# A decoder block's delta-rule inverse: the product of its steps in a piece of the attention's memory instead of a scratch tile

## The chip, the cores and the metric

The kernel runs on one core of a Trainium2 chip. The metric is the device time of one launch in microseconds (us). Engines go by these names: TensorE (PE; PEld is its weight load), VectorE (DVE), ScalarE (ACT), GpSimd (POOL) and SyncE (SP, which issues most DMAs).

## The reference

One decoder block on x [256, 1024] in float32: one wide input projection, a gated delta rule (8 heads of 128, chunks of 64 tokens), a sparse attention with compressed, selected and windowed keys (8 query heads, 2 key heads), a gated merge of the two branches, a layer norm, a gated feed-forward with a causal convolution, and a second layer norm. The part that the change touches is the delta rule's triangular solve:

```python
lower = jnp.where(strict, jnp.einsum('nbhid,nbhjd->nbhij', k_beta, k) * decay, 0.0)
a_mat = lower + jnp.eye(C, dtype=jnp.float32)
rhs = jnp.concatenate([v_beta, k_beta * jnp.exp(g)[..., None]], -1)
sol = lax.linalg.triangular_solve(a_mat, rhs, left_side=True, lower=True, unit_diagonal=True)
```

There are 32 matrices `a_mat` (8 heads, 4 chunks) of 64x64. `v` comes from a causal convolution of four taps over the tokens and a SiLU.

## The kernel before

**Weight chunks.** The whole block is a list of weight chunks of 128x1024 (`plan`, from `head_plan`): first those of `k`, `q`, the compression and the attention's keys and queries, then eight each of `v`, `z`, `mgd`, `mgn`, `wd`, `wn`, `wo`, then the feed-forward. SyncE loads them into six `raw` buffers (L170). Each is split into a rounded part `hi` (a cast on ScalarE, L192) and a remainder `lo` (a subtraction on VectorE, L197; for a few early chunks partly on GpSimd); up to three split chunks are held. `mm_feat` (L319 to L321) multiplies a chunk of projection weights in 24 matmuls, three for each of eight 128-row slices: hi by the high half of the input, hi by its low half, lo by the high half. The result goes into a PSUM tile `pg`, of which there are two.

**What follows a `v` chunk.** `feat` multiplies and then calls `evac_v` (from L1049). It takes a scratch tile `cv` (`scr`, three buffers of 128x512 that go round in the order of the requests), and `conv` fills it: the last tap is a scaled copy on ScalarE (L146, `cv<-pg`), the three others are multiply-adds on VectorE (L351), all reading `pg`. A deferred SiLU on ScalarE then writes `cv` into `Z` (`Z<-cv`, L146). After that `feat` splits the next chunk (`ahead`) and gives every open side stream one step (`pump`).

**Side streams.** The delta rule (`delta`), the attention and others are Python generators. Each runs until it yields, and the numbers in `W` and `WAITS` say for how many chunks it does. So the order of instructions on each engine is fixed when the program is written; an engine that waits holds all that stands behind it in its queue. Waits between engines come from the tiles that the instructions read and write.

**The inverse.** `delta` inverts the diagonal 16x16 blocks of all matrices at once by substitution on GpSimd. The blocks are brought into a layout with one block row per partition by a write to DRAM and a read back (L571, L573). Then 15 steps follow, each a product into `tmp` (L581) and a subtraction from the inverse `Xi` (L583); the largest product has 8x8 = 64 elements per partition. A copy makes the transpose (L586). Two writes to DRAM (L589) and two reads (L592), transpose first, bring both into the layout for TensorE. Four masked copies each on ScalarE (L146, `LT<-VN`) and VectorE (L602) spread them into the block-diagonal `TT` (transpose, first) and `T`. From there TensorE doubles the blocks to 32 and 64: `pa` (L615, reads `L` and `TT`), `pu` (L621) and `pt` (L626). `tmp` is a scratch tile of the same three buffers, named `itmp`:

```python
tmp = self.scr("itmp")
...
t = tmp[:, :n * m].rearrange("p (r c) -> p r c", r=n)
nc.gpsimd.tensor_tensor(t, Ln[:, j + 1:16, j:j + 1].to_broadcast([128, n, m]),
                        Xi[:, 0, j:j + 1, 0:m].to_broadcast([128, n, m]), op=OP.mult)
nc.gpsimd.tensor_tensor(Xi[:, 0, j + 1:16, 0:m], Xi[:, 0, j + 1:16, 0:m], t, op=OP.subtract)
```

The requests for scratch tiles around it are, in this order: `hp` (L784, the first compression's result), `itmp`, `hp` (the second's), and one `cv` for each of the eight `v` chunks.

**AT.** A tile of 128x4608 that many parts use in turn: at first the input, then columns 0 to 4095 as slots for the compression's weight chunks (L239), the columns from 4096 on as slots for the squares of `q` and `k` (`norm_sq`), and later the attention's weights, in 0 to 4515 (`EE`, `PT`, `e6`, `er`).

Of the kernel before, what the change touches and what calls it, by code (L numbers as in the profile page):

```python
# [99 lines left out]
class Body:  # L100
# [363 lines left out]
    def delta(self):  # L464
# [106 lines left out]
        nc.gpsimd.dma_start(sl.rearrange("u p j -> p u j"), Lc)  # L571
        yield from self.wait("lw")
        nc.gpsimd.dma_start(vf[:, 256:512], sl.rearrange("u (b i) j -> (u b) (i j)", b=8))  # L573
        tmp = self.scr("itmp")
        nc.vector.memset(Xi[:, 0], 0.0)
        nc.vector.memset(vf[:, 512:768:17], 1.0)
        yield from self.wait("inv")
# [945 lines left out]
```

## Time and profile before

| what | us |
|---|---|
| median of 3 runs | 573.6 (573.47 to 574.25) |
| the profiled execution, device time | 573.08 |
| its span in the profile | 571.3 |
| TensorE busy | 554.5 (97%) |
| VectorE busy | 394.1 (69%) |
| ScalarE busy | 306.7 (54%) |
| GpSimd busy | 110.3 (19%) |

Times in the profile count from the span's start. A row of a timeline is: start, duration, engine, line, operation, output<-inputs with shapes, and in brackets the idle time of the engine ahead of it with what ended that. A wait for several engines is put down to the one that the profile shows last. Consecutive matmuls overlap, so a matmul of 0.28 us starts 0.12 us after the one ahead of it. A row of windows has the stretch, its length, then busy time and number of instructions of PE, PEld, DVE, ACT and POOL, the granted clock, the DMA engines' busy share and GB/s. [...]

### The profile page before, as it was taken

To read this page: it belongs to the slowest core of one execution; us is meant where nothing else is said; L and a number is where in the kernel's file an instruction comes from. 1 tells how busy PE (TensorE), PEld (TensorE's weight loads), DVE (VectorE), ACT (ScalarE), POOL (GpSimd) and SP (SyncE) were. 2 spreads that over 40 slices of the span, in tenths; PEclk is the share of its full clock that TensorE was granted. 3 is DMA by queue.
4 is the path that set the end of the run, shared out by engine and by line. 5 is a ranking of instruction groups with operands and counts; after the bars stand their busy time and mean duration, and the time that the engine had idled before them with its cause. 6 is when DMAs were issued, how large, how long until landed. Compare 5 with 4: busy or idle time off the path is not lost.

```text
span 571.3 us, 11612 instructions
## 1 busy us (share of the span) xinstructions
PE 554.5 (97%) x4585; PEld 508.8 (89%) x4585; DVE 394.1 (69%) x683; ACT 306.7 (54%) x575; POOL 110.3 (19%) x160
## 2 busy tenths in 40 slices
PE   8999999999799999999999999999999999999994
PEld 6999999988798898888898898899999999999974
DVE  2888745766686563467657487788777777778884
ACT  4656544624464446564677344465655555556651
POOL 2466632017401130004001000068000000000003
PEclk9999999999899999999999999999999999999998
DMA  8985548765552233223354645735655555555601
GB/s 317 406 305 180 190 146 278 287 211 185 145 182 93 76 112 111 76 73 112 112 185 128 242 148 183 258 102 180 209 185 191 191 180 192 186 189 172 200 3 73
DMA packets 28182, 99.94 MB, mean 175 GB/s; under 512 B 3340, under 2 KB 3996, under 8 KB 27740
## 3 DMA queue, kind: packets, MB, share of 16 engines
q1 hardware_dynamic: 27312, 95.94, 49.1%
q0 software_dynamic: 672, 2.93, 1.7%
q8 instruction: 36, 0.59, 0.4%
q10 hardware_dynamic: 144, 0.33, 0.1%
q14 instruction: 18, 0.15, 0.1%
HBM read 97.33 MB, written 1.46 MB: 173 GB/s over the span
## 4 chain that ended last, share of the span: by engine, by line
PE 77%; DVE 9%; ACT 6%; POOL 3%; issue 2%; DMA 2%; POOLq 0%; SPq 0%; DVEq 0%; ACTq 0%
PE pg L319 18%; PE pg L321 17%; PE pg L320 17%; PE pdn L1284 3%; PE pdn L1285 3%; PE pdn L1283 3%; DVE lo L197 2%; ACT hi L192 2%; PE poa L959 2%; PE pwo L1002 1%; PE pwo L1001 1%; PE pwo L1000 1%; ACT AT L146 1%; POOL itmp L581 1%; POOL VN L583 1%
## 5 line engine op out<-in xcount | busy, mean ns | idle before, releaser
L197 DVE TENSOR_TENSOR lo<-raw,hi 128x1024 fp32r<-128x1024 f32 (+1 forms) x147 | 179.2, 1221 | 75.3 <-ACT hi L192 74.4
L192 ACT CAST hi<-raw 128x1024 fp32r<-128x1024 f32 (+1 forms) x151 | 154.6, 1028 | 36.5 <-PE pg L320 9.8
L319 PE MATMUL pg<-X,hi 128*128 128x256 f32 x496 | 144.3, 291 | 4.8 <-ACT cv L146 4.8
L321 PE MATMUL pg<-X,lo 128*128 128x256 f32 x496 | 140.3, 283 | 0.0
L320 PE MATMUL pg<-X,hi 128*128 128x256 f32 x496 | 140.2, 283 | 0.0
L319 PE MATMUL pg<-Y,hi 128*128 128x256 f32 x400 | 113.0, 283 | 0.0
L320 PE MATMUL pg<-Y,hi 128*128 128x256 f32 x400 | 112.7, 282 | 0.0
L321 PE MATMUL pg<-Y,lo 128*128 128x256 f32 x400 | 112.5, 281 | 0.0
L319 PEld LDWEIGHTS pg<-X,hi 128*128 128x128 f32 x496 | 94.1, 190 | 9.7 <-ACT cv L146 4.9
L320 PEld LDWEIGHTS pg<-X,hi 128*128 128x128 f32 x496 | 94.2, 190 | 0.3 <-issue 0.2
L321 PEld LDWEIGHTS pg<-X,lo 128*128 128x128 f32 x496 | 94.1, 190 | 0.1
L320 PEld LDWEIGHTS pg<-Y,hi 128*128 128x128 f32 x400 | 75.3, 188 | 0.3 <-issue 0.2
L319 PEld LDWEIGHTS pg<-Y,hi 128*128 128x128 f32 x400 | 75.3, 188 | 0.2 <-issue 0.2
L321 PEld LDWEIGHTS pg<-Y,lo 128*128 128x128 f32 x400 | 75.3, 188 | 0.0
L351 DVE SCALAR_TENSOR_TENSOR cv<-pg,ppk,cv 128x255 f32<-128x255 f32 (+2 forms) x72 | 34.6, 481 | 17.4 <-ACT cv L146 15.7
L1359 POOL TENSOR_TENSOR NQ<-NQ,AT 128x512 f32<-128x512 f32 x2 | 2.6, 1298 | 159.7 <-ACT NQ L146 159.7
L1284 PE MATMUL pdn<-lo,X 128*128 128x512 f32 (+1 forms) x90 | 31.6, 351 | 0.0
L1283 PE MATMUL pdn<-hi,X 128*128 128x512 f32 (+1 forms) x90 | 31.5, 350 | 0.0
L1285 PE MATMUL pdn<-hi,X 128*128 128x512 f32 (+1 forms) x90 | 31.4, 349 | 0.0
L910 POOL TENSOR_SCALAR AT<-AT,sums 128x128 f32<-128x128 f32 (+1 forms) x12 | 10.9, 918 | 95.3 <-DVE ec L903 48.4
L351 DVE SCALAR_TENSOR_TENSOR uv<-pg,ppk,uv 128x255 f32<-128x255 f32 (+1 forms) x44 | 21.2, 481 | 11.3 <-ACT uv L146 10.1
L146 ACT ACTIVATE cv<-pg,ppk 128x256 f32<-128x256 f32 x24 | 11.4, 474 | 32.2 <-PE pg L321 26.4
(353 smaller groups left out, 925.8 us busy)
## 6 DMA issues: line engine op xcount, KB each, us to landing
raw<-in_w SPq DMA_DIRECT2D x156, 512.0 KB, 3.4
AT<-in_w SPq DMA_DIRECT2D x12, 512.0 KB, 6.4
Z<-in_w SPq DMA_DIRECT2D x4, 512.0 KB, 7.8
AT<-in_first SPq DMA_DIRECT2D x3, 512.0 KB, 6.6
V<-in_xk POOLq DMA_DIRECT2D x1, 1024.0 KB, 5.5
KD<-in_lnp POOLq DMA_DIRECT2D x1, 1024.0 KB, 6.8
AT<-in_lnp SPq DMA_DIRECT2D x1, 1024.0 KB, 8.1
AT<-in_first SPq DMA_DIRECT2D x2, 256.0 KB, 3.4
```

Source lines behind the costliest of these rows:

```text
L146: self.nc.scalar.activation(out, in_, func, **kw)
L192: nc.scalar.copy(hi[:, o:o + n], raw[:, o:o + n])
L197: nc.vector.tensor_tensor(lo[:, :n], raw[:, :n], hi[:, :n].bitcast(F32), op=OP.subtract)
L319: nc.tensor.matmul(pg, hi[:, k], src[:, 0, k], start=(k == 0), stop=False)
L320: nc.tensor.matmul(pg, hi[:, k], src[:, 1, k], start=False, stop=False)
L321: nc.tensor.matmul(pg, lo[:, k], src[:, 0, k], start=False, stop=(k == 7))
L351: nc.vector.scalar_tensor_tensor(dst[:, s:], pg[:, :S - s], cw[:, n - 1 - s:n - s], dst[:, s:], op0=OP.mult, op1=OP.add)
L910: (nc.vector, nc.gpsimd)[b].tensor_scalar(e, e, w, None, op0=OP.mult)
L959: nc.tensor.matmul(po, self.VT[:, b % 2, c0:c0 + 128], PT[:, b].rearrange("p i q -> p (i q)"), start=False, stop=(b == bs[-1]))
L1283: nc.tensor.matmul(p, fh[:, ts], hi[:, sl], start=(j == 0), stop=False)
L1284: nc.tensor.matmul(p, fh[:, ts], lo[:, sl], start=False, stop=False)
L1285: nc.tensor.matmul(p, fl[:, ts], hi[:, sl], start=False, stop=(j == NFF - 1))
```

## The change

The product of each step is no longer put in a scratch tile but in columns 4516 to 4579 of AT. Nothing else is changed in the source.

```diff
         nc.gpsimd.dma_start(vf[:, 256:512], sl.rearrange("u (b i) j -> (u b) (i j)", b=8))
-        tmp = self.scr("itmp")
+        tmp = self.AT[:, 4516:4580]
         nc.vector.memset(Xi[:, 0], 0.0)
```

Instructions stay in the same order on all engines; some waits differ. On ScalarE, this is the place of the first two `v` chunks. The row names are line, operation, output<-input, shape and the engines or DMA queues that the instruction waits for. Before:

```order
L785 COPY hp<-ph 128x256 [waits PE_49]
L146 ACTIVATE cv<-pg,ppk 128x256 [waits PE_49]
L192 CAST hi<-raw 128x1024 [waits DMAHW6_49,DVE_49]
L146 ACTIVATE hex_1778<-phs 128x60 [waits PE_49]
L141 ACT_TABLE_LOAD
L146 ACTIVATE cv<-pg,ppk 128x256 [waits PE_49,Pool_49]
L192 CAST hi<-raw 128x1024 [waits DMAHW7_49,DVE_49]
```

Now:

```order
L785 COPY hp<-ph 128x256 [waits PE_49]
L146 ACTIVATE cv<-pg,ppk 128x256 [waits PE_49]
L192 CAST hi<-raw 128x1024 [waits DMAHW6_49,DVE_49]
L146 ACTIVATE hex_1777<-phs 128x60 [waits PE_49]
L141 ACT_TABLE_LOAD
L146 ACTIVATE cv<-pg,ppk 128x256 [waits PE_49]
L192 CAST hi<-raw 128x1024 [waits DMAHW7_49,DVE_49]
```

The second `cv`, of the second `v` chunk, no longer waits for GpSimd. Further down ScalarE's queue stand the four masked copies of the inverse; this is the difference there:

```order
 L146 ACTIVATE cv<-pg,ppk 128x256 [waits PE_49,Activation_49]
 L192 CAST hi<-raw 128x1024 [waits DMAHW6_49]
-L146 ACTIVATE LT<-VN,cpk 128x16x16 [waits DMASW4_49,DMASW7_49,DMASW2_49,DMASW1_49]
+L146 ACTIVATE LT<-VN,cpk 128x16x16 [waits DMASW4_49,DMASW2_49,DMASW7_49,DMASW1_49,Pool_49]
 L146 ACTIVATE LT<-VN,cpk 128x16x16
 L146 ACTIVATE LT<-VN,cpk 128x16x16 [waits DMASW0_49]
```

The first of them now names GpSimd as well as the reads from DRAM, which GpSimd issues itself after its steps. On GpSimd, the first two steps are, as a difference:

```order
 L571 DMA lscr<-VN 128x16x16 [waits DVE_49,Activation_49]
 L573 DMA VN<-lscr 128x256 [waits DMASW3_49,PE_49]
-L581 TENSOR_TENSOR itmp<-VN 128x15 [waits DMASW4_49,DVE_49]
-L583 TENSOR_TENSOR VN<-VN,itmp 128x15 [waits PE_49,Pool_49]
+L581 TENSOR_TENSOR AT<-VN 128x15 [waits DMASW4_49,DVE_49]
+L583 TENSOR_TENSOR VN<-VN,AT 128x15 [waits PE_49,Pool_49]
```

Only the place of the product differs; the waits are the same.

## Rows read from the trace of the kernel before

**Rows 1.** TensorE's waits: waiter, releaser, us in total, times, longest.

```profile
PE pg L319 <- ACT cv L146: 4.8, 1, 4.8
PE pg L328 <- DMA AT<-in_first: 1.1, 1, 1.1
```

**Rows 2.** Timeline of TensorE, end of v2 and start of v3.

```profile
142.04 0.28 PE L321 MATMUL pg<-X,lo 128*128 128x256 f32 x1
147.07 0.55 PE L319 MATMUL pg<-X,hi 128*128 128x256 f32 x1 [4.76 <-ACT cv L146]
...
150.20 0.36 PE L321 MATMUL pg<-X,lo 128*128 128x256 f32 x1
150.39 0.29 PE L319 MATMUL pg<-X,hi 128*128 128x256 f32 x1
```

**Rows 3.** Windows: stretch, its length, busy us of each engine, granted clock, DMA share.

```profile
142.10:147.07 4.97, 0.22 (x2) 0.04 (x2) 1.59 (x4) 2.17 (x5) 3.88 (x12) 0.99 0.24 97
147.07:150.39 3.32, 3.32 (x15) 3.32 (x16) 3.25 (x5) 1.17 (x2) 2.24 (x2) 0.51 0.56 179
150.39:153.20 2.81, 2.81 (x26) 2.81 (x25) 1.30 (x3) 1.47 (x3) 0.84 (x3) 1.00 0.92 178
```

**Rows 4.** Timeline of ScalarE, beside the gap.

```profile
137.76 1.28 ACT L141 ACT_TABLE_LOAD   x1
144.90 0.47 ACT L146 ACTIVATE cv<-pg,ppk 128x256 f32<-128x256 f32 x1 [5.86 <-POOL VN L583]
```

**Rows 5.** Timeline of GpSimd, steps of the inverse.

```profile
138.03 0.31 POOL L583 TENSOR_TENSOR VN<-VN,itmp 128x63 f32<-128x63 f32 x1
138.42 1.17 POOL L581 TENSOR_TENSOR itmp<-VN 128x64 f32<-128x64 f32 x1
...
144.65 0.22 POOL L583 TENSOR_TENSOR VN<-VN,itmp 128x15 f32<-128x15 f32 x1
```

**Rows 6.** Timeline of VectorE, beside the gap.

```profile
138.15 1.27 DVE L197 TENSOR_TENSOR lo<-raw,hi 128x1024 fp32r<-128x1024 f32 x1
...
140.31 0.22 DVE L803 TENSOR_TENSOR hid<-phs,hex 128x60 f32<-128x60 f32 x1
145.41 1.52 DVE L351 SCALAR_TENSOR_TENSOR cv<-pg,ppk,cv 128x255 f32<-128x255 f32 x3 [4.88 <-ACT cv L146]
146.84 1.22 DVE L197 TENSOR_TENSOR lo<-raw,hi 128x1024 fp32r<-128x1024 f32 x1
```

**Rows 7.** Timeline of ScalarE, steady stretch and the copies of the inverse.

```profile
157.42 0.47 ACT L146 ACTIVATE cv<-pg,ppk 128x256 f32<-128x256 f32 x1 [1.12 <-PE pg L321]
...
160.27 0.48 ACT L146 ACTIVATE cv<-pg,ppk 128x256 f32<-128x256 f32 x1 [1.12 <-PE pg L321]
...
161.58 1.71 ACT L146 ACTIVATE LT<-VN,cpk 128x256 f32<-128x256 f32 x4
```

**Rows 8.** SyncE's weight loads: two issues of the timeline, and landing of all.

```profile
139.45 0.33 SPq L170 DMA_DIRECT2D raw<-in_w  x1
148.09 0.33 SPq L170 DMA_DIRECT2D raw<-in_w  x1
DMA to landing us min/median/max: 3.1/3.4/10.1
```

**Rows 9.** GpSimd's read-back L592: the two issues in the timeline, and landing.

```profile
148.15 2.33 POOL L592 DMA_DIRECT2D VN<-tscr  x2 [1.19 <-DMA tscr<-VN]
...
DMA to landing us min/median/max: 4.9/5.3/5.7
```

**Rows 10.** Timeline of VectorE, copies of the inverse and taps of v7.

```profile
163.35 1.13 DVE L602 TENSOR_SCALAR LT<-VN,cpk 128x256 f32<-128x256 f32 x4
164.40 1.50 DVE L351 SCALAR_TENSOR_TENSOR cv<-pg,ppk,cv 128x255 f32<-128x255 f32 x3
```

**Rows 11.** Timeline of TensorE, `pa` and the second `z` chunk.

```profile
165.79 1.15 PE L615 MATMUL pa<-LT 64*64 64x64 f32 x32
168.87 0.36 PE L319 MATMUL pg<-X,hi 128*128 128x256 f32 x1
```

## The prediction

> **What bounds the kernel now.** I read four views. The page's first part has TensorE busy for nearly the whole span, so only what makes TensorE wait or slows its matmuls can move the time. The waits of TensorE come next [rows 1]: one wait of 4.8 us stands out, and the next longest is 1.1 us, at the program's start. The timeline of TensorE places it: the last matmul of the third `v` chunk (I count the eight `v` chunks v0 to v7) starts at 142.04, the first of v3 at 147.07 [rows 2]. [...] Fourth, the other engines beside the gap. ScalarE's bias-free copy of v1 (`cv`) waits 5.86 us for GpSimd's L583 and starts at 144.90 [rows 4], right after GpSimd's last step of the inverse, which ends at 144.65 + 0.22 = 144.87 [rows 5]. VectorE's three conv taps for v1 follow at 145.41 and end at 146.93, after VectorE had idled 4.88 us [rows 6]; v3 starts 0.14 us later. The profile names ScalarE as TensorE's releaser, but `cv` had ended at 145.37: the tap on VectorE is what came last, because v3's product goes into the PSUM tile (two of them) that v1's taps read.
>
> So the chain is: GpSimd's last step, `cv` of v1, its taps, v3. The link between the first two is no data. v1's `cv` is the third scratch tile after `itmp` (after `hp` of the second compression and v0's `cv`), so with three buffers it lies in `itmp`'s memory.
>
> **The change, step by step.** The 30 steps on GpSimd stay, in the same order and of the same sizes; no instruction moves on any engine. Taking one tile out of the rotation puts v1 in the buffer of the first `hp` and v2 in that of the second, both read long before. The order shows v1's `cv` waiting for TensorE alone, and GpSimd's first step waiting for the same two things as before; columns 4516 to 4579 of AT touch neither the weight slots (below 4096) nor the attention's parts (to 4515), and the squares that also used them belong to the `k` and `q` chunks.
>
> *Term 1, the gap.* v1's matmuls end with v2's start, one chunk before 142.16, at about 139.3 plus the 0.28 us of the last one [rows 2]. ScalarE's table load ends at 139.04 [rows 4]. So `cv` of v1 runs at 139.5 and takes 0.47. VectorE is the later one: before v1's taps stand in its queue the lo of 138.15 and the small operations that end at 140.31 + 0.22 = 140.53 [rows 6]. From there the taps take 1.52, to 142.05; with the 0.14 us seen before, v3 may start at 142.2. v2 would let it start 0.12 us after 142.04, at 142.16. The gap closes within 0.1 us: 147.07 - 142.16 = 4.91 us.
>
> *Term 2, the clock.* 15 matmuls took 3.32 us at the low level [rows 3]. At full speed 24 take the 2.85 us between two `cv` of the steady stretch (157.42 and 160.27) [rows 7], 0.119 each, so 15 take 1.78. Gain 1.54 us. It goes with the idle time that came ahead of it.
>
> *Term 3, what then follows.* After v3 each chunk needs 2.85 us on TensorE; VectorE needs 1.52 + 1.22 = 2.74 per chunk [rows 6]. Carrying VectorE's queue on from 142.05 gives v2's taps done at 144.65, with v4 due at 145.01, and v3's at 147.25, with v5 due at 147.86: it keeps up, by 0.4 us at the tightest. Weights are not late: after the four issues up to 139.45 the next waits until 148.09, just as the lo of 146.84 frees a buffer, and a load lands in 3.4 us at the median [rows 8], against a lead of about four chunks. These transfers will simply start about 5 to 6 us sooner, with VectorE. Cost: nothing, up to 0.3 us.
>
> *Term 4, GpSimd loses quiet.* Today VectorE idles from 140.5 to 145.4 and GpSimd's steps run undisturbed. Now lo operations fall at about 142.0, 144.6 and 147.2. How GpSimd fares beside a lo the trace shows: the step of 138.42 under the lo of 138.15 took 1.17 us, its neighbour 0.31 [rows 5]: 0.86 more for one lo. Two lo operations before the end of the steps make the inverse 1.7 us later, three (the copy behind it too) 2.6. The read-back is issued at 148.15 for the transpose and 1.17 later, at 149.32, for the other, and lands 4.9 and 5.7 us after the issue [rows 9]: 153.05 and 155.0 now, 154.8 and 156.7 then (155.7 and 157.6 with three). Its readers come 6.45 us sooner: ScalarE's first four-piece copy at 155.1, the other half at 156.0 [rows 7], VectorE's at 156.9 [rows 10]. So ScalarE waits about 0.7 us for the second half (1.6 with three). v7's `cv` lies behind it, and its taps end 0.3 us (1.2) late; but the next chunk to need that PSUM tile starts at 168.87, 3.0 us after v7's taps end at 165.90 today [rows 10, 11]. TensorE needs the transpose for `pa` at 165.79, 1.9 us after VectorE's two copies of it (half of 1.13 us behind 163.35) [rows 10, 11]. I take a loss of 0 here, bounded by 0 and 1.6.
>
> [...]
>
> **Sum.** 4.91 + 1.54 = 6.45 us. The profiled execution took 573.08 us (span 571.3, 1.8 around it), so 566.6 by its own clock. It lies 0.5 us below the median of the runs shown, 573.6; the median gives 573.6 - 6.4 = 567.2 us, which I take.
>
> **Rivals.**
>
> *The inverse becomes the wait (part of the gain).* For: the slack of its readers shrinks from 8.5 us (153.05 to 161.58) to about 0.3 [rows 7, 9]. Against: v7's taps and `pa` have 3.0 and 1.9 us to spare. If three lo hold GpSimd and DMA issues are delayed on top, so that 1 to 2.4 us reach TensorE, the time is 568.2 to 569.6.
>
> *Nothing gained.* The new piece of AT or another tile of the rotation holds v1's `cv` for as long, or v3 waits for something else until 147. Then 573.6. Against: the order's waits, the free buffers, the lo of v3 done at 139.42 [rows 6], loads well ahead.
>
> *Slower: the late inverse stops TensorE at `pa`.* The place is the 32 products of L615. The transpose's copies on VectorE have 156.9 - 153.05 = 3.85 us of slack to landing, and 1.9 more to `pa`: from 5.7 us of delay of the inverse on, TensorE waits. A new wait of some 5 us brings the low clock back, 1.54. Delay must then reach 5.7 + 6.45 - 1.54 = 10.6 us to cancel the gain, 11.8 to be 1.2 us slower, 574.8. After 142.0 GpSimd has 8 steps, a copy and 4 DMA issues left; all 13 held by 0.86 would be 11.2. But a lo covers only 1.22 of every 2.85 us, so it would need GpSimd's DMA issues to suffer far more than its steps. Against that: the two issues from 148.15 took 1.17 each beside today's lo operations [rows 9].
>
> [...]
>
> **How the numbers follow.** A measurement of this kernel tells about 0.2%, 1.15 us, from no change. Full gain: 0.80, at 566.2 to 568.2 (the terms' own roundings and term 3's 0.3 to one side, the spread of 573.47 to 574.25 to the other). Part of the gain: 0.13, mostly 568.2 to 569.6. Nothing gained: 0.04. Slower: 0.03. The range 566.2 to 569.6 takes the first two, stretched by term 4's bound. Faster 0.80 + 0.13 = 0.93, same 0.04, slower 0.03.
>
> **What would show it.** Right: TensorE's 4.8 us wait gone, no clock below 0.95 between 130 and 160 us, `cv` of v1 near 139.5, v3's first matmul near 142.2, `pa` near 159.3, and everything after it 6.4 us earlier. GpSimd's steps should end near 146 to 147 instead of 144.9, with two or three of them lasting about 1.2 us, and ScalarE's copies from VN should show a wait for a DMA below 2 us. Wrong: a wait of `pg` L319 that remains, `pa` waiting for VectorE or ScalarE, or a later stall that takes the 6.4 us back.

## The result and the profile after

The changed kernel took 569.26 us (median of 4 runs, 568.89 to 569.38) against 573.88 us for the kernel before, run beside it: a ratio of 0.9916 with a 95% interval of 0.9901 to 0.9932, 4.6 us less. It was run once more, unaltered, beside the later experiments: 569.62 us, ratio 0.9925 (0.9912 to 0.9939). The forecast was 567.2, with a range of 566.2 to 569.6. So the sign and the range held; about two microseconds of the forecast gain are missing. The two profiled executions lie only 3.7 us apart (569.38 against 573.08, which is 0.8 us below the median of the runs beside the change), so the traces below have to account for 2.7 us that are missing.

First the place of the gap. TensorE's timeline, end of v2 and start of v3 [rows 2], and the window over the stretch where the clock had fallen to 0.51 [rows 3]; the window's columns are its length, busy time of PE, PEld, DVE, ACT and POOL, granted clock (TensorE's, as a share of full speed), DMA share and GB/s:

```profile
142.04 0.28 PE L321 MATMUL pg<-X,lo 128*128 128x256 f32 x1
142.15 0.29 PE L319 MATMUL pg<-X,hi 128*128 128x256 f32 x1
```

```profile
140.00:150.00 10.00, 10.00 (x87) 10.00 (x85) 9.38 (x17) 6.42 (x11) 7.38 (x17) 1.00 0.75 254
```

v3 starts at 142.15 instead of 147.07, and the clock stays at full speed (1.00). The two engines ahead of it, ScalarE [rows 4] and VectorE [rows 6]:

```profile
139.51 0.48 ACT L146 ACTIVATE cv<-pg,ppk 128x256 f32<-128x256 f32 x1 [0.46 <-PE pg L321]
```

```profile
140.29 0.22 DVE L803 TENSOR_TENSOR hid<-phs,hex 128x60 f32<-128x60 f32 x1
140.43 1.51 DVE L351 SCALAR_TENSOR_TENSOR cv<-pg,ppk,cv 128x255 f32<-128x255 f32 x3
141.85 1.22 DVE L197 TENSOR_TENSOR lo<-raw,hi 128x1024 fp32r<-128x1024 f32 x1
142.99 1.51 DVE L351 SCALAR_TENSOR_TENSOR cv<-pg,ppk,cv 128x255 f32<-128x255 f32 x3
144.41 1.28 DVE L197 TENSOR_TENSOR lo<-raw,hi 128x1024 fp32r<-128x1024 f32 x1
```

ScalarE's `cv` of v1 now waits for TensorE's product, and VectorE goes on to the taps without a pause, behind the small operations that were queued there.

Then what became late. GpSimd's steps and read-back [rows 5, 9], with the landing of the write L589 and of the read-back L592:

```profile
141.95 1.27 POOL L583 TENSOR_TENSOR VN<-VN,AT 128x55 f32<-128x55 f32 x1
...
144.69 1.10 POOL L581 TENSOR_TENSOR AT<-VN 128x28 f32<-128x28 f32 x1
...
146.48 0.22 POOL L583 TENSOR_TENSOR VN<-VN,AT 128x15 f32<-128x15 f32 x1
...
147.69 1.12 POOL L589 DMA_DIRECT2D tscr<-VN  x2 [0.30 <-POOL VN L586]
151.79 2.35 POOL L592 DMA_DIRECT2D VN<-tscr  x2 [2.98 <-DMA tscr<-VN]
```

```profile
L589 POOL DMA_DIRECT2D tscr<-VN x2: 545/566/586, 147.7 to 148.3; - x2
...
DMA to landing us min/median/max: 3.8/4.0/4.2
...
L592 POOL DMA_DIRECT2D VN<-tscr x2: 1162/1166/1171, 151.8 to 153.0; - x2
...
DMA to landing us min/median/max: 4.5/5.3/6.0
```

The last step ends at 146.70 instead of 144.87: beside each of the two lo of 141.85 and 144.41 one step took longer (1.27 and 1.10 us) and ended just after the lo. The write of the inverse then landed 3.8 to 4.2 us after its issue; in the kernel before it was 2.0 us, so the read-back is issued 3.64 us later than before (148.15). ScalarE [rows 7] and VectorE [rows 10] meet it at the copies:

```profile
156.43 0.91 ACT L146 ACTIVATE LT<-VN,cpk 128x256 f32<-128x256 f32 x2 [1.20 <-DMA VN<-tscr]
159.03 0.91 ACT L146 ACTIVATE LT<-VN,cpk 128x256 f32<-128x256 f32 x2 [1.69 <-DMA VN<-tscr]
...
160.15 0.45 ACT L146 ACTIVATE cv<-pg,ppk 128x256 f32<-128x256 f32 x1
```

```profile
159.03 0.62 DVE L602 TENSOR_SCALAR LT<-VN,cpk 128x256 f32<-128x256 f32 x2 [1.53 <-DMA VN<-tscr]
160.63 1.52 DVE L351 SCALAR_TENSOR_TENSOR cv<-pg,ppk,cv 128x255 f32<-128x255 f32 x3 [0.99 <-ACT cv L146]
```

The four copies of one engine stood in one row before; now each half waits for its DMA, 2.9 us in all on ScalarE. v7's `cv`, behind them, comes at 160.15; 6.45 us before its old place would be 157.05. TensorE [rows 11] and its waits [rows 1]:

```profile
159.34 1.15 PE L615 MATMUL pa<-LT 64*64 64x64 f32 x32
...
165.78 0.70 PE L889 MATMUL psa<-KC,NQ 128*128 128x256 f32 x2 [0.28 <-DVE A L617]
...
173.09 1.36 PE L552 MATMUL pv<-cpk,Z 128*128 128x128 f32 x8 [1.10 <-ACT AT L146]
177.54 1.15 PE L615 MATMUL pa<-LT 64*64 64x64 f32 x32 [0.24 <-DVE LT L628]
...
182.21 0.70 PE L889 MATMUL psa<-KC,NQ 128*128 128x256 f32 x2 [1.03 <-DVE A L617]
```

```profile
PE psa L889 <- DVE A L617: 1.3, 2, 1.0
PE pv L552 <- ACT AT L146: 1.1, 1, 1.1
```

The first `pa` is 6.45 us earlier than before, 159.34 against 165.79. Then four short stalls of 0.28, 1.10, 0.24 and 1.03 us follow, 2.65 together, where the kernel before had one of 0.6. Of 6.45 us, 2.7 were given back between 165 and 185 us, and the place where they went is VectorE's first `A` (L617), which TensorE's `psa` waits for. These are `A` and the last `pa`, first before and then now:

```profile
168.79 0.68 DVE L617 TENSOR_TENSOR A<-pa,cpk 128x512 f32<-128x512 f32 x1
202.32 1.15 PE L615 MATMUL pa<-LT 64*64 64x64 f32 x32
```

```profile
165.04 0.68 DVE L617 TENSOR_TENSOR A<-pa,cpk 128x512 f32<-128x512 f32 x1
198.58 1.15 PE L615 MATMUL pa<-LT 64*64 64x64 f32 x32
```

Both are 3.7 us earlier than before, as is the span (567.6 against 571.3). `A` stands in VectorE's queue behind v7's taps, and with 6.45 us it would have come at 162.34: it is 2.70 us late, as the taps are (160.63 against 164.40 - 6.45 = 157.95). In the kernel before, in the change and in e5 the last `pa` starts 33.5 us after the first `A` (in e5 196.16 against 162.63), while the first `pa` lies 3.0 us ahead of `A` in the first and in e5, and 5.7 us in the change. So here TensorE's time follows `A`, and the stalls are how TensorE falls back to it.

### The profile page after: what moved, and what is told of

It reads as the page before. It is cut to its first block, busy times and chain, and to the rows that moved or that the text cites. A ratio compares the mean times of both kernels' runs of the same rounds, so it can differ in the third digit from the quotient of the medians.

```text
span 567.6 us, 11611 instructions
## 1 busy us (share of the span) xinstructions
PE 553.5 (98%) x4585; PEld 507.5 (89%) x4585; DVE 394.2 (69%) x683; ACT 307.0 (54%) x575; POOL 112.4 (20%) x160
## 3 DMA queue, kind: packets, MB, share of 16 engines
HBM read 97.33 MB, written 1.46 MB: 174 GB/s over the span
## 4 chain that ended last, share of the span: by engine, by line
PE 81%; DVE 8%; ACT 6%; issue 2%; DMA 1%; POOL 1%; POOLq 0%; SPq 0%; DVEq 0%; ACTq 0%
PE pg L319 19%; PE pg L320 18%; PE pg L321 18%; PE pdn L1284 3%; PE pdn L1285 3%; PE pdn L1283 3%; DVE lo L197 2%; ACT hi L192 2%; PE poa L959 2%; PE ph L780 1%; PE pwo L1002 1%; PE pwo L1001 1%; PE pwo L1000 1%; ACT AT L146 1%; DMA AT<-in_first 1%
## 5 line engine op out<-in xcount | busy, mean ns | idle before, releaser
L1323 ACT CAST X<-ug 128x256 fp32r<-128x256 f32 x22 | 8.9, 407 | 33.2 <-DVE ug L1319 33.2
```

Source lines behind the costliest of these rows:

```text
L1323: nc.scalar.copy(fh, f)
```

## The experiments

The theory: freeing the scratch tile removes the gap and the low clock, and the rest is given back because the inverse comes back later from DRAM, held by lo operations and by weight loads that now run beside its DMAs. The rivals: AT's place has an effect of its own; the clock's share was hidden anyway; the loss is something else. The runs e1 to e4 were made beside the kernel before on one chip (573.97 us there), e5 to e8 beside it on another (573.83).

### The product in another free place (e1, repeated as e8)

```diff
-        tmp = self.scr("itmp")
+        tmp = vf[:, 768:832]
```

> The product of the steps lies in columns 768 to 831 of VN (the half of the inverse's own tile that is only written after the steps) instead of AT; the scratch rotation is as in the change. Theory (freeing the scratch tile is all that counts, where the product lies does not): 569.3 us within 0.5, GpSimd's last step at about 146.7, the read-back's wait of about 3 us, TensorE stalls of about 1.8 to 2.7 us between 160 and 185 us. Rival (AT's place has a cost or gain of its own, by its traffic with the weight loads): more than 1 us away from 569.3 and other stalls.

Measured: 570.48 us, ratio 0.9939 (0.9923 to 0.9954), 1.2 us above the change's first time and so outside the expected band, by as much as the rival asked for. The profiled execution, the fastest of the six (568.55), had stalls of only 0.2 and 0.8 us, with a write that landed after 3.3 to 3.4 us. Since the change had not been timed beside this run, both ran again side by side.

> The product in VN's free half once more, beside the change on the same chip, since its first run was 1.2 us slower than the change's own. Theory (place does not matter): equal to the change within 0.4 us. Rival (VN's place costs about 1 us): 1 us slower than the change in this call too.

> The change itself, unaltered, on the same chip as the other runs of this call. Expected: 569.3 within 0.6 us, 0.8% below the kernel before.

Measured: 569.63 us for VN's half (0.9928, 0.9912 to 0.9944) and 569.62 for the change. Between these two places no difference shows; the 1.2 us of the first run were not repeated. TensorE's waits in the second run of VN's half, from 170 to 182 us, show the same stalls as the change (one of 0.2 us at `psa` comes before them):

```profile
PE pv L552 <- ACT AT L146: 1.1, 1, 1.1
PE psa L889 <- DVE A L617: 1.0, 1, 1.0
PE pa L615 <- DVE LT L628: 0.3, 1, 0.3
```

### The gap kept, the clock held up (e2)

```diff
     def feat(self, kind, idx, src, evac):
+        if (kind, idx) == ("v", 3):
+            pw = self.ps("pw")[0:64]
+            for _ in range(20):
+                self.nc.tensor.matmul(pw, self.nc.const_aps.tensor(1.0, [128, 64], BF),
+                                      self.nc.const_aps.tensor(1.0, [128, 512], BF), start=True, stop=True)
         pg = self.mm_feat(*self.next_chunk(kind, idx), src)
```

> The kernel before, with 20 idle products of constants on TensorE ahead of v3, so that the wait for v1's taps stays but TensorE is busy in it. Their results are not used. Theory (terms 1 and 2 are separate: 4.9 us of gap and 1.54 us of low clock behind it): the clock stays at 1.00 after 147 us, v3 starts at about 147.1 as before, and the time falls by 1.5 us to about 572.3, less 0.3 if the products run over the wait's end. Rival (the low clock's 1.5 us is hidden by what follows, VectorE's queue or the inverse): no change, 573.9. Third: the idle products hold a PSUM tile and shift other waits: slower than 574.2.

Measured: 571.79 us, ratio 0.9963 (0.995 to 0.9977), 2.2 us less, with 1.3 to 2.9 by the interval. The timeline of TensorE and the window over the stretch after the gap:

```profile
142.59 4.54 PE L339 MATMUL pw<-const-bfloat16-1.0 128*64 128x512 bf16 x20
147.41 0.36 PE L319 MATMUL pg<-X,hi 128*128 128x256 f32 x1 [0.28 <-ACT cv L146]
```

```profile
147.10:150.40 3.30, 3.02 (x26) 3.03 (x26) 3.23 (x6) 1.47 (x3) 2.10 (x3) 1.00 0.53 150
```

v3 still starts after v1's taps (all of this run is 0.33 us later from its start: GpSimd's last step ends at 145.20 instead of 144.87), but the granted clock is 1.00 and 26 matmuls (25 of v3 and the end of the last idle product) stand in a stretch that held 15. v6's `cv` comes at 159.14 instead of 160.27; with the 0.33, 1.46 us gained. The second term is separate from the first and of the size that was worked out, and what follows does not swallow it.

### T's copies one chunk later (e4)

```diff
                 if b % 2:
                     self.act(o, tc, AF.Copy, scale=bm[:, b:b + 1])
                 else:
                     nc.vector.tensor_scalar(o, tc, bm[:, b:b + 1], None, op0=OP.mult)
+            if w:
+                yield
```

The wait behind the copies (`lev0`) is one shorter, so that `pa` stays in its place.

> The change, with the two copies of T on ScalarE and the two on VectorE moved one chunk later in the queues, behind v7's cv and taps; the copies of TT and pa stay where they are. Theory (the loss of 2 us is the wait for the second half of the read-back, which holds v7's cv and with it VectorE's queue): cv of v7 at about 157.5 instead of 160.15, TensorE's stalls between 160 and 185 us fall to about 0.6 us as before, 567.3 to 568.0 us. Rival (the loss is the lateness of T or TT for the products themselves, or comes from elsewhere): 569.3 within 0.4.

Measured: 568.29 us, ratio 0.9899 (0.9881 to 0.9916): 1.0 to 1.3 us below the change's two times, but the intervals overlap. ScalarE's timeline:

```profile
158.27 0.91 ACT L146 ACTIVATE LT<-VN,cpk 128x256 f32<-128x256 f32 x2 [1.82 <-DMA VN<-tscr]
...
159.39 0.46 ACT L146 ACTIVATE cv<-pg,ppk 128x256 f32<-128x256 f32 x1
160.68 0.91 ACT L146 ACTIVATE LT<-VN,cpk 128x256 f32<-128x256 f32 x2
```

The second half is waited for no more. But the first half landed later in this run (read-back 5.5 us after its issue or more), and it still holds v7's `cv`: this run lies 1.2 us behind the change from its start (last step ending at 147.92), so 159.39 stands for 158.2, 2.0 us better than 160.15, not the 2.65 expected. TensorE's stalls from 158 to 206 us are 0.2 and 0.8, 1.0 together where the change had 2.65 (0.6 was expected). The direction is the theory's, the size between the two.

### Weight loads kept away (e3 and e5)

```diff
             nc.gpsimd.dma_start(vf[:, 256 * w:256 * w + 256].rearrange("p (u j) -> p u j", j=16),
                                 st[w].rearrange("u p j -> p u j"))
+        yield
+        nc.sync.dma_start(self.dram.tile([1, 16], F32, name="gate"), vf[0:1, 0:16])
         yield from self.wait("back")
```

This is e5, with `back0` one shorter; in e3 the same DMA is deferred by one load more. SyncE's queue stops at it until the read-back has landed.

> The change, plus a 64-byte DMA on SyncE's queue that reads the inverse after its read-back from DRAM and stands ahead of the weight load of 145.7: that load and the next ones start only at about 155 us, long before their chunks are due (about 167 us). Theory (the inverse's write took 4.0 us instead of 2.0 because it shares the DMA engines with weight loads): the write lands 2.0 us after its issue, the read-back is issued at about 150.0, ScalarE's wait ahead of the LT copies falls from 2.9 to below 1 us, TensorE's stalls at psa and pv shrink, 567.3 to 567.9 us. [...] Third (the burst of held loads is late or slows the read-back): above 569.3.

Measured: 567.38 us, ratio 0.9884 (0.9866 to 0.9901). The landing times of the write and the read-back, and ScalarE's copies:

```profile
L589 POOL DMA_DIRECT2D tscr<-VN x2: 547/566/586, 148.3 to 148.9; - x2
...
DMA to landing us min/median/max: 3.4/3.5/3.6
...
L592 POOL DMA_DIRECT2D VN<-tscr x2: 1159/1165/1171, 152.2 to 153.4; - x2
...
DMA to landing us min/median/max: 3.8/3.9/4.0
```

```profile
156.37 1.72 ACT L146 ACTIVATE LT<-VN,cpk 128x256 f32<-128x256 f32 x4 [0.39 <-DMA VN<-tscr]
...
158.30 0.46 ACT L146 ACTIVATE cv<-pg,ppk 128x256 f32<-128x256 f32 x1
```

The time came out as expected, but not by the step that was named. The write was still slow: a load had left SyncE at 146.35, ahead of the held ones, and the write of 148.32 met it. What became quick is the read-back, 3.8 to 4.0 us with no load beside it. So the run could not tell whether the loads or the lo operations beside it made the write slow, and the gate was put one load earlier.

> As the run that holds the weight loads, with the gate one load earlier, so that the load of 145.7 stays back too and neither the inverse's write nor its read-back meets a weight load. Theory (both DMAs of the inverse are slowed by the weight loads that now run beside them): the write lands 2.0 us after its issue (3.5 with the later gate, 4.0 in the change), the read-back 3.8 to 4.0 (5.3 in the change); ScalarE's LT copies wait for nothing or below 0.3 us; 566.8 to 567.4 us, the full 6.5 us below the kernel before. Rival (GpSimd's write is slow beside VectorE's lo operations, not beside loads): write 3.5 or more again, 567.4 or above.

Measured: 567.23 us, ratio 0.9885 (0.9869 to 0.99). SyncE's queue, the landing times, ScalarE's copies and TensorE's wait:

```profile
143.38 0.33 SPq L170 DMA_DIRECT2D raw<-in_w  x1
156.21 0.30 SPq L595 DMA_DIRECT2D gate<-VN  x1
156.61 1.30 SPq L170 DMA_DIRECT2D raw<-in_w  x3
```

```profile
L589 POOL DMA_DIRECT2D tscr<-VN x2: 545/566/586, 148.0 to 148.5; - x2
DMA to landing us min/median/max: 2.7/2.9/3.0
L592 POOL DMA_DIRECT2D VN<-tscr x2: 1162/1168/1173, 151.2 to 152.4; - x2
DMA to landing us min/median/max: 3.8/3.8/3.8
```

```profile
155.41 1.73 ACT L146 ACTIVATE LT<-VN,cpk 128x256 f32<-128x256 f32 x4
...
157.34 0.45 ACT L146 ACTIVATE cv<-pg,ppk 128x256 f32<-128x256 f32 x1
```

```profile
PE psa L891 <- DVE A L619: 0.6, 1, 0.6
```

ScalarE's copies wait for nothing, v7's `cv` stands where the sum had put it (157.05, and this run is 0.27 us later from its start), and of the four stalls one of 0.6 us is left, as in the kernel before. By the same 0.27 us, the first of the held loads left 10.6 us later than in the change and the fifth 1.2 us later; TensorE waited for none of them. So the loss was the late inverse, and keeping the weight loads away from its two DMAs makes it good.

It does not follow that the loads were the larger part of the lateness. In the change the read-back was issued 3.64 us later than before, of which 1.83 are GpSimd's steps and 1.8 the write; the read-back itself took about as long as before (4.5 and 6.0 us against 4.9 and 5.7, both beside loads). With the loads away it is issued only 0.8 us earlier than in the change (by the same 0.27 us), while its second half lands 2.2 us sooner after its issue: most of what this run wins back comes from a read-back faster than that of the kernel before.

The write took 2.7 to 3.0 us without loads, not the 2.0 of the kernel before. The lo beside its issue (147.50 to 148.76) did not hold up its start: by the trace's DMA packets its first one moved 1.16 us after the issue (149.13), as in the kernel before (147.00). But one other transfer ran beside it, a packet of 16 KB that the profile calls instruction; this is its row in the DMA view from 148 to 150 us (packets, MB, share of 16 engines):

```profile
q8 instruction: 1, 0.02, 3.2%
```

That share is 1.0 us on one of the 16 engines. The write's last packets moved from 150.20 to 150.80, with 0.06 of the DMA engines busy, about one of 16. In the kernel before, with 2.0 us, no such packet fell beside the write (145.8 to 148.5 us); in the change, with 3.8 to 4.2 us, one did (147.7 to 152). So the packet fits the last 0.9 us, but no run moved it, and this is not shown.

### Both (e6)

> The quiet run and the later T copies together. Theory (both cure the same wait): no better than the quiet run alone, within 0.4 us of it. Rival (they cure different losses): 0.5 us or more below both.

Measured: 566.94 us, ratio 0.9876 (0.986 to 0.9892), against 567.23: the same within the measurement, as the theory had it. Once the inverse is in time, moving T's copies adds nothing that shows. e5 and e6 are the fastest versions here, 6.6 and 6.9 us below the kernel before and some 2.4 to 2.7 below the change.

## Why the prediction was right, and where it fell short

**The chain** was read rightly: the only link between GpSimd and v1's `cv` was the buffer. The order said that the wait goes, and e1 and e8 show that another free place does the same.

**Term 1** gave 4.91 us; v3 starts 147.07 - 142.15 = 4.92 us earlier. VectorE was the later of the two engines ahead of it, with the taps at 140.43 (140.53 forecast).

**Term 2** gave 1.54 us; e2 showed 1.46 in its trace, by itself.

**Term 3** held: `pa` is exactly 6.45 us earlier (159.34), VectorE kept up, no weight was late.

**Term 4** is the step that failed: "I take a loss of 0 here, bounded by 0 and 1.6." Its first half was right. Two lo operations fell on the steps and cost 0.98 and 0.86 us (1.27 against 0.29, 1.10 against 0.24); the last step ends 1.83 us later, against 1.7. What I left out is the DMAs: I moved the write and the read-back along with their durations of before, 2.0 and 4.9 to 5.7 us, although term 3 said that the weight loads move forward by 5 to 6 us. In the kernel before the same stall that held TensorE had also emptied the DMA queues (no load was issued from 139.45 to 148.09 [rows 8], and from 144.0 to 146.8 the DMA engines' share was 0.00), so the 2.0 us were those of a write with no load beside it. With loads and the instruction packet beside it the write took 4.0; the read-back kept about its durations. The halves therefore landed at about 156.3 and 159.0 instead of 154.8 and 156.7, and the wait on ScalarE was 2.9 us instead of 0.7. The loss was 2.7 us by the traces; the bound of 1.6 was too low for the same reason and for the next one.

The second part of term 4 that failed is the slack: I measured it at v7's PSUM tile (3.0 us) and at `pa` (1.9). Both held, `pa` was not late. The queue behind was the nearer limit: v7's taps on VectorE came at 160.63 instead of 157.95, `A` (L617), further back in VectorE's queue, came late with them, and TensorE's `psa` waited for it. On that path there was no slack: the taps' 2.68 us came through whole, and by the 33.5 us from `A` to the last `pa`, which hold in the kernel before as well, the 0.3 us that term 4 let the taps be late would have cost 0.3 us too.

**The rivals.** "The inverse becomes the wait" is what happened, with 0.13 given to it and 568.2 to 569.6 us as its place. The measured 569.26 lies there and not in the place of the full gain (566.2 to 568.2, given 0.80), so the range held by its second outcome, and in part by luck: what that rival asked for, three lo on GpSimd and late DMA issues, did not come. No row shows the 1 us at the low end of its 1 to 2.4 us; the traces show 2.7 us lost. The third lo, of 147.22, met only the end of the copy, which took 0.64 us against 0.61. "Nothing gained" and "slower" did not occur; GpSimd's DMA issues took 0.55 to 0.59 and 1.16 to 1.17 us each as before, so no issue was held.

How the two steps fared beside a lo: that of 141.95 ended at 143.22 where the lo of 141.85 ended at 143.07, that of 144.69 at 145.79 where the lo of 144.41 ended at 145.69. Each step lasted until the lo was over. When it started, 1.12 and 1.00 us of the lo were left, and it cost 0.98 and 0.86 us, less than the lo's own 1.22 and 1.28. Why a step lasts longer beside a lo, no run shows.

## What to carry to other kernels

A tile that a slow side engine uses as scratch belongs in no rotation with tiles on the main path; the price of sharing is a wait without data (here 4.9 us), and behind it, as here, a stretch at the low clock (0.51 for 3.3 us, 1.5 us lost). When a stall is removed, take no duration from the time of the stall: what ran beside it was slower when the work moved in, here two steps on GpSimd (1.27 and 1.10 us beside a lo, 0.29 and 0.24 before) and a DMA write (4.0 us with loads and a packet beside it, 2.0 before). For slack, follow the whole queue behind the late instruction, not only its direct reader.

## What the runs showed that was not expected

A 128 KB write from GpSimd's queue, which landed 2.0 us after its issue in the kernel before, where the DMA engines had been idle from 144.0 to 146.8, took 3.3 to 4.2 us beside 512 KB weight loads (e1: 3.3 to 3.4; the change: 3.8 to 4.2) and still 2.6 to 3.0 without them (e5, e6; in e5 only the instruction packet ran beside it). The read-back took 4.4 to 6.2 us beside loads (e7: 4.4 to 5.9; e2: 5.8 to 6.2) and 3.8 to 4.0 without (e3, e5, e6). Holding the loads back, the first by 10.6 us, was worth 2.4 us, and no stall of TensorE came of it.
